# Norm factors of a retention and HGRN2 layer: spread by transposes of a step-zero column in place of products of ones with diagonals

## The chip, the cores and the metric

The kernel runs on one core of one Trainium2 chip. The metric is the device time of one execution in microseconds; the median of several runs counts.

## The reference

One decoder layer for a prompt of 2048 tokens and for 8 decode rows, model width 1024, all in f32. Cut to what matters:

```python
def rmsnorm(x, g):
    y = x * lax.rsqrt(jnp.mean(x * x, axis=-1, keepdims=True) + NORM_EPS)
    return y * g

h = rmsnorm(x, norm_g)                       # one factor per token, one gain per column
p = h @ w_in                                 # 1024 x 4096
rq, rk, rv, rg, hq, hf, hi, hgate = jnp.split(p, 8, axis=-1)
# retention: rotary on rq and rk, fixed decay per head, 4 heads of 128
# HGRN2: forget gate from hf and hg_lb, 4 heads of 128
# both: chunkwise recurrence, norm per head, times silu of the gate
y = x + concat([o_ret, o_hg]) @ w_out
y_prompt, y_sample = rmsnorm(y, final_norm_g)      # and the new states
```

The edited code deals with the factor `rsqrt(mean(x*x) + eps)` of the first norm.

## The kernel before, in words

**Blocks.** The prompt is cut into 8 blocks of 256 tokens, in the order `V_ORDER = [4, 5, 6, 7, 2, 3, 0, 1]`. A first phase runs over `TOK`: the 8 blocks three times, for three sets of weight columns. Its step `i` works on block `TOK[i]`. Steps 0 and 1 are plain products, whose outputs are scaled with the factors; from step 2 on `v_pair(i, after)` computes seven products of a Strassen-like scheme (`PRODUCTS`, `CHAIN`) on sums of input and weight quarters. Every f32 product is made of three on a high and a low part (`three`), and `hi_lo` makes these parts: ScalarE copies the high part (L115), VectorE subtracts it (L116). Later phases (the projections `pj`, the scan and the output projection) are not edited.

**The factors.** The tokens' squares are summed by ScalarE (`stats_sum`, tiles `xn`), and GpSimd makes the factors out of them (`stats_end`, `rsqrt_mean`, L111 and L112): `rs_all` holds them with the 128 tokens of a half block on the partitions, one column for each half block. The input `x_t`, however, lies with the model width on the partitions and the tokens along the row. To scale it, each factor must stand on all 128 partitions, along the row. This is the spread:

- `spread_dg(i)`: VectorE scales the identity with each of the block's two factor columns (L288), into two diagonals `dg` in a buffer `rk`.
- `spread(i)`: TensorE multiplies a matrix of ones with each diagonal (L293), into a PSUM tile `prs`; VectorE copies that to `rb` (L295).
- `tok_ops(i)`: VectorE multiplies the raw input with the gain and with `rb` (L313), `hi_lo` splits it into the operands `ab_h` and `ab_l`, the sums `S` for the scheme are made, and the scaled input and sums are stored (`a_dram`, `s_dram`) for the later steps.

Blocks that a step finds stored (`spooled`) need no spread: eight steps have one, i = 2 to 7, 10 and 11. The spread of step `i + 1` runs while step `i` computes: the diagonals after its first product, the products with ones after its second.

The 8 decode rows have the same in small: `decode_dg` makes an 8x8 diagonal `dgd` (L621), `decode_spread` multiplies ones with it (L625, tile `prsd`). The decode gates' products (`wg_decode`, tiles `pgd`, L600) stand in steps 2 to 5 and use raw weights `wgr` that SyncE's queue loads (L527).

**Order.** Only TensorE runs in the order in which the program writes its instructions:

```python
with tile.TileContext(nc) as tc, tc.manual_schedule(engines={mybir.EngineType.PE}):
```

The order on the other engines and on the DMA queues is planned when the program is built. `behind(f)` and `tc.issue_after` tie some pieces to what stands before them: `past(i, f)` issues the diagonals behind the last VectorE instruction of the block's split (`lows[i]`). Most loads and stores go through SyncE's one queue. The lists `after[n]` say after which product of a step a piece of side work is written.

The query transposes `q_flip` (L470, tile `pqt`) are ordinary transposes on TensorE, four for each half block, and are left as they are.

Of the kernel before, what the change touches and what calls it, by code (L numbers as in the profile page):

```python
# [10 lines left out]
F32 = mybir.dt.float32  # L11
# [3 lines left out]
ALU = mybir.AluOpType  # L15
# [3 lines left out]
P = 128  # L19
# [4 lines left out]
NB = 8  # L24
NH = 4
CH = HALF // P
GW = 512
# [14 lines left out]
def step_kernel(ctx, tc, a, out):  # L42
    nc = tc.nc
    pe, act, dve, pool, sp = nc.tensor, nc.scalar, nc.vector, nc.gpsimd, nc.sync

    const = ctx.enter_context(tc.tile_pool(name="const", bufs=1))
    sm = ctx.enter_context(tc.tile_pool(name="sm", bufs=2))
# [27 lines left out]
    ident = const.tile([P, P], F32, name="ident")  # L75
    make_identity(nc, ident)
    ones = const.tile([P, P], F32, name="ones")
# [27 lines left out]
    rs_all = const.tile([P, T // P], F32, name="rs_all")  # L105
    rsd = const.tile([NB, 2], F32, name="rsd")
# [7 lines left out]
    def hi_lo(h, l, src):  # L114
        act.activation(h, src, AF.Copy)  # L115
        dve.tensor_tensor(l, src, h.bitcast(F32), op=ALU.subtract)  # L116
# [7 lines left out]
    def behind(f):  # L124

        last = {}
        for i in reversed(nc.cur_bb.bb.instructions):
            if i.engine in (dve.engine, act.engine, sp.engine) and i.engine not in last:
                last[i.engine] = i
                if len(last) == 3:  # L130
                    break
        with ExitStack() as es:
            for i in last.values():
                es.enter_context(tc.issue_after(i))
            f()
# [63 lines left out]
    TOK = V_ORDER + [1, 2, 4, 5, 3, 6, 7, 0] + list(range(8))  # L199
    N_V = len(V_ORDER)  # L200
    vctx = ExitStack()
    vq = vctx.enter_context(tc.tile_pool(name="vq", bufs=1))
# [43 lines left out]
    def spooled(i):  # L246
        return i >= 2 * N_V or (i >= N_V and TOK[i] not in TOK[:2])

    def same(i):
        return 0 < i < len(TOK) and TOK[i] == TOK[i - 1]  # L250

    def slot(i):
        return (i - sum(same(n) for n in range(i + 1))) % 2
# [25 lines left out]

    spread_to = {}  # L280

    dgs = {}

    def spread_dg(i):
        t = vq.tile([P, GW], F32, tag="rk", name=f"dg{i}")
        dgs[i] = [t[:, :P], t[:, P : 2 * P]]
        for dg, c in zip(dgs[i], (2 * TOK[i], 2 * TOK[i] + 1)):
            dve.tensor_scalar(dg, ident, rs_all[:, c : c + 1], None, op0=ALU.mult)  # L288

    def spread(i):  # L290
        pt = ps_tr.tile([P, 2, P], F32, tag="tr", name=f"prs{i}")
        for j, dg in enumerate(dgs[i]):
            pe.matmul(pt[:, j], ones, dg, start=True, stop=True)  # L293
        dst = vq.tile([P, GW], F32, tag="rq", name=f"rb{i}")[:, :256]
        dve.tensor_copy(dst, pt.rearrange("p a b -> p (a b)"))  # L295
        spread_to[i] = dst

    sop, lows = {}, {}

    def past(i, f):  # L300
        if i not in lows:
            return f()
        with tc.issue_after(lows[i]):
            f()

    def tok_ops(i, held=None):
        store = held.append if held is not None else lambda f: f()
        r0, r1 = xr[i]
        for j, r in enumerate((r0, r1)):
            if not spooled(i):  # L310
                for k in range(4):
                    kk = 4 * j + k
                    dve.scalar_tensor_tensor(  # L313
                        r[:, k], r[:, k], g_in[:, kk : kk + 1], spread_to[i], op0=ALU.mult, op1=ALU.mult
                    )
            kk = slice(4 * j, 4 * j + 4)
            bb = (slice(3 * slot(i), 3 * slot(i) + 1), slice(3 * slot(i) + 1, 3 * slot(i) + 3))[j]
            ra = r.rearrange("p k (o t) -> p o k t", t=P)[:, : 1 + j]
            hi_lo(ablk[0][:, bb], ablk[1][:, bb], ra)
            if not spooled(i):  # L320
                store(lambda kk=kk, r=r: sp.dma_start(a_dram[TOK[i]][:, kk], r))
        if spooled(i):
            return
        lows[i] = next(x for x in reversed(nc.cur_bb.bb.instructions) if x.engine == dve.engine)
        a11, a21, a12, a22 = r0[:, :, :P], r0[:, :, P:], r1[:, :, :P], r1[:, :, P:]
        ta, tb = (rawp.tile([P, 2, 4, P], F32, tag="raw", name=f"S{n}_{i}") for n in range(2))
        s2, s3, s1, s4 = ta[:, 0], ta[:, 1], tb[:, 0], tb[:, 1]
        dve.tensor_tensor(s1, a21, a22, op=ALU.add)
        dve.tensor_tensor(s2, s1, a11, op=ALU.subtract)
        dve.tensor_tensor(s3, a11, a21, op=ALU.subtract)  # L330
        dve.tensor_tensor(s4, a12, s2, op=ALU.subtract)
        sraw[i] = (ta, tb)
        for n, t in enumerate(sraw[i]):
            store(lambda n=n, t=t: sp.dma_start(s_dram[TOK[i]][n], t))
# [3 lines left out]
    def s_split(i, m):  # L338
        hl = split(sraw[i][m].rearrange("p s k t -> p (s k t)"), f"s{i}{m}")
        for n, op in enumerate((("S2", "S3"), ("S1", "S4"))[m]):  # L340
            sop[i, op] = [
                x[:, n * 512 : n * 512 + 512].rearrange("p (k t) -> p k t", k=4) for x in hl
            ]
# [175 lines left out]
    def wv_comb(k):  # L519
        for op, r in w_sums(wr[k], wr[k + 4]):  # L520
            h, l = wv(op, k)
            hi_lo(h, l, r)
# [92 lines left out]
            dve.tensor_scalar(t, t, rsd[:, ty : ty + 1], None, op0=ALU.mult)  # L615
            sp.dma_start(vd_dram[ty], t)

    dgd = sm.tile([NB, NB], F32, tag="dgd", name="dgd", bufs=1)

    def decode_dg():  # L620
        dve.tensor_scalar(dgd, ident[:NB, :NB], rsd[:, 1:2], None, op0=ALU.mult)  # L621

    def decode_spread():
        pt = ps_tr.tile([P, NB], F32, tag="tr", name="prsd")
        pe.matmul(pt, ones[:NB, :], dgd, start=True, stop=True)  # L625
        rb = sm.tile([P, NB], F32, tag="rbd", name="rbd", bufs=1)
        act.activation(rb, pt, AF.Copy)
        dve.tensor_tensor(xs, xs, rb.unsqueeze(1).to_broadcast([P, KT, NB]), op=ALU.mult)
# [61 lines left out]
    tok_load(2)  # L690
    wv_comb(2)
    wv_comb(3)
    spread_dg(2)
    for ty in (1, 0):
        for c in range(2):
            ps = bank([P, GW], f"pv1{c}{ty}")
# [21 lines left out]
    rk, rb_of = {}, {}  # L718
# [199 lines left out]
    for i in range(2, n_tok):  # L918
        after = {n: [] for n in range(7)}
        m, j = i // N_V + 1, i % N_V  # L920
# [11 lines left out]
        if same(i + 1):  # L932
            for op in ("S1", "S2", "S3", "S4"):
                sop[i + 1, op] = sop[i, op]
        elif i + 1 < n_tok:
            if not spooled(i + 1):
                after[0] += [lambda i=i: past(i, lambda: spread_dg(i + 1))]
                after[1] += [lambda i=i: spread(i + 1)]
            tied = behind if i >= N_V - 1 else lambda f: f()
            late = 2 if same(i) else 0  # L940
            after[2 + late] += [
                lambda i=i, t=tied: t(lambda: tok_ops(i + 1)), lambda i=i, t=tied: t(lambda: s_split(i + 1, 0))
            ]
            after[4 + late // 2] += [lambda i=i, t=tied: t(lambda: s_split(i + 1, 1))]
# [11 lines left out]
            after[4] += [lambda i=i: rot_load(i + 1)]  # L956
        if i == 2:
            after[3] += [lambda: behind(decode_values_out)]
            after[0] += [decode_dg]
            after[2] += [decode_spread]  # L960
        if m < 3:
            if 2 <= j < 6:
# [727 lines left out]
    def op_load(i):  # L1690
        oraw[i] = [rawp.tile([P, 8, P], F32, tag="raw", name=f"or{c}") for c in (2 * i, 2 * i + 1)]
        for c, r in zip((2 * i, 2 * i + 1), oraw[i]):
            sp.dma_start(r, o_dram[:, :, c * P : (c + 1) * P].rearrange("h p t -> p h t"))
# [12 lines left out]
    def op_s12(i):  # L1706
        a11, a12, a21, a22 = op_views(i)
        ta, tb = (rawp.tile([P, 2, 4, P], F32, tag="raw", name=f"oS{n}_{i}") for n in range(2))
        osum[i] = (ta, tb)
        dve.tensor_tensor(tb[:, 0], a21, a22, op=ALU.add)  # L1710
        dve.tensor_tensor(ta[:, 0], tb[:, 0], a11, op=ALU.subtract)

    def op_s34(i):
        a11, a12, a21, a22 = op_views(i)
        ta, tb = osum[i]
        dve.tensor_tensor(ta[:, 1], a11, a21, op=ALU.subtract)  # L1716
        dve.tensor_tensor(tb[:, 1], a12, ta[:, 0], op=ALU.subtract)
# [11 lines left out]
    def op_a(i):  # L1729
        op_pair(i, oraw[i][0], "A11", "A12")  # L1730
# [148 lines left out]
    for n in range(4):  # L1879
        i, st_ = ((4, 0), (4, 4), (5, 0), (5, 4))[n]  # L1880
        wd_at[i] += [(st_, lambda n=n: wd_load(2 * n)), (st_, lambda n=n: wd_load(2 * n + 1))]
        i, st_ = ((4, 3), (5, 0), (5, 4), (6, 1))[n]
# [5 lines left out]
    for i in range(p0, n_pairs):  # L1888
        after = {}
        if i + 1 < n_pairs:  # L1890
            after = {
                0: [lambda i=i: op_load(i + 1)],
                1: [lambda i=i: op_a(i + 1)],
                2: [lambda i=i: op_s12(i + 1)],
                3: [lambda i=i: op_s34(i + 1)],
                4: [lambda i=i: op_s23(i + 1)],
                5: [lambda i=i: op_s14(i + 1), lambda i=i: xr_load(i + 1)],
                6: [lambda i=i: op_a22(i + 1)],
            }
# [88 lines left out]
```

## Time and profile before

| | |
|---|---|
| median of 3 runs | 1039.06 us (1038.57 to 1042.16) |
| the profiled execution | 1038.73 us, span 1037.0 us |
| TensorE busy | 1023.4 us (99%), weight loads 849.9 us (82%) |
| VectorE busy | 746.6 us (72%) |
| ScalarE busy | 556.5 us (54%) |
| GpSimd busy | 129.0 us (12%) |
| moved by DMA | 255.61 MB, mean 247 GB/s |
| diagonals on VectorE (L288) | 16, 0.265 to 0.289 us each, at 46.3 to 221.9 us |
| products with ones (L293) | 32 records, 0.272 to 0.275 us each, at 49.7 to 227.8 us |

Rows of the timeline give the start, the duration, the engine, the line, the operation, the output and the inputs, and the number of merged instructions; in brackets stands the engine's idle time before it and what ended that. PE is TensorE, PEld its weight loads, DVE VectorE, ACT ScalarE, POOL GpSimd, SP SyncE; a q behind the name is the engine's queue. The durations on TensorE overlap, since it is pipelined: the time that an instruction takes from the stream is seen in the start times. A row of a group by line or tile gives the least, the median and the largest duration in ns. A row of the list of waits gives who waited for whom, the total in us, how often, and the longest.

### The profile page before, as it was taken

What the parts mean: (1) busy time and instruction counts of PE and PEld (TensorE: products, weight loads), DVE (VectorE), ACT (ScalarE), POOL (GpSimd) and SP (SyncE); (2) the same over time, 40 slices, a digit from 0 to 9 for tenths busy, and PEclk for the clock granted to TensorE, in tenths of its full rate; (3) what the DMA queues carried; (4) which work ended last, traced back from release to release, by engine and by line L of the source; (5) the groups of instructions that cost most, each with busy time, mean ns of one, the idle gap of its engine ahead of it and who ended that gap; (6) DMA issues with size and microseconds to landing.
All of it is one profiled execution on the core that took longest, in us unless ns stands there. A gap on an engine that the chain in (4) does not pass through costs nothing. (4 is left out here: it accounts for less than half of the span.)

```text
span 1037.0 us, 21324 instructions
## 1 busy us (share of the span) xinstructions
PE 1023.4 (99%) x8231; PEld 849.9 (82%) x8231; DVE 746.6 (72%) x1387; ACT 556.5 (54%) x1217; POOL 129.0 (12%) x231
## 2 busy tenths in 40 slices
PE   9999999999999999999999999999999999999997
PEld 7777778887778888888888889898888878888775
DVE  6886676887666876666665767768768577667886
ACT  7863346644445765545554756566656465433232
POOL 0310001000000111111111100111012102311122
PEclk9999999999999999999999999999999999999999
DMA  8699999779998975586885686745783395575652
GB/s 295 217 326 327 341 326 314 272 250 328 316 333 295 374 241 162 161 276 210 238 256 163 244 313 225 257 138 187 230 266 122 118 370 203 178 271 190 238 184 102
DMA packets 151270, 255.61 MB, mean 247 GB/s; under 512 B 11424, under 2 KB 79280, under 8 KB 151040
## 3 DMA queue, kind: packets, MB, share of 16 engines
q1 hardware_dynamic: 143584, 229.22, 65.6%
q0 software_dynamic: 7440, 24.76, 6.2%
q8 instruction: 65, 1.06, 0.4%
q14 instruction: 37, 0.30, 0.1%
q10 hardware_dynamic: 144, 0.26, 0.1%
HBM read 166.51 MB, written 87.69 MB: 245 GB/s over the span
## 5 line engine op out<-in xcount | busy, mean ns | idle before, releaser
L1235 ACT ACTIVATE kepth<-kh 128x1024 f32<-128x1024 f32 x24 | 25.5, 1061 | 70.4 <-DVE kh L1225 70.4
L1039 PE MATMUL pjfh<-xh,w_h 128*128 128x512 f32 (+2 forms) x160 | 59.5, 372 | 0.0
L1039 PE MATMUL pjqh<-xh,w_h 128*128 128x512 f32 (+2 forms) x160 | 59.0, 368 | 0.0
L1039 PE MATMUL pjqh<-xh,w_l 128*128 128x512 f32 (+2 forms) x160 | 55.7, 348 | 0.0
L1039 PE MATMUL pjfh<-xl,w_h 128*128 128x512 f32 (+2 forms) x160 | 55.7, 348 | 0.0
L1039 PE MATMUL pjqh<-xl,w_h 128*128 128x512 f32 (+2 forms) x160 | 55.6, 347 | 0.1
L1039 PE MATMUL pjfh<-xh,w_l 128*128 128x512 f32 (+2 forms) x160 | 55.6, 348 | 0.0
L1225 DVE TENSOR_TENSOR kh<-kh,fph 128x512 f32<-128x512 f32 x48 | 33.3, 695 | 23.0 <-PE plh L1255 13.2
L116 DVE TENSOR_TENSOR ab_l<-xr,ab_h 128x512 fp32r<-128x512 f32 (+1 forms) x40 | 37.5, 954 | 7.1 <-ACT ab_h L115 6.8
L782 DVE SCALAR_TENSOR_TENSOR obr<-por,omr,rg 128x128 f32<-128x128 f32 x64 | 18.0, 344 | 32.4 <-POOL omr L774 32.4
L772 ACT ACTIVATE obr<-por 128x128 f32<-128x128 f32 x64 | 16.9, 278 | 43.2 <-PE por L759 40.9
L115 ACT ACTIVATE ab_h<-xr 128x512 fp32r<-128x512 f32 (+1 forms) x40 | 32.4, 840 | 13.6 <-DVE xr L313 13.6
L419 ACT ACTIVATE vo<-vo 128x512 f32<-128x512 f32 x32 | 20.1, 630 | 27.3 <-DVE vo L413 13.4
L1039 PEld LDWEIGHTS pjqh<-xh,w_h 128*128 128x128 f32 x160 | 30.4, 190 | 4.6 <-issue 1.2
L1039 PEld LDWEIGHTS pjfh<-xh,w_h 128*128 128x128 f32 x160 | 30.2, 189 | 4.1 <-issue 0.4
L1039 PEld LDWEIGHTS pjqh<-xh,w_l 128*128 128x128 f32 x160 | 30.1, 188 | 4.2 <-issue 0.3
L1039 PEld LDWEIGHTS pjfh<-xh,w_l 128*128 128x128 f32 x160 | 30.1, 188 | 4.0
L1228 DVE TENSOR_TENSOR qqh<-qqh,fph 128x512 f32<-128x512 f32 x48 | 32.8, 684 | 0.0
L1039 PEld LDWEIGHTS pjqh<-xl,w_h 128*128 128x128 f32 x160 | 30.2, 189 | 2.9
L1039 PEld LDWEIGHTS pjfh<-xl,w_h 128*128 128x128 f32 x160 | 30.2, 189 | 2.7
L313 DVE SCALAR_TENSOR_TENSOR xr<-xr,g_in,rb 128x256 f32<-128x256 f32 x64 | 27.1, 480 | 7.1 <-issue 4.3
L1666 PE MATMUL py<-woh,oc_h 128*128 128x512 f32 x64 | 26.7, 417 | 0.0
(1840 smaller groups left out, 3383.1 us busy)
## 6 DMA issues: line engine op xcount, KB each, us to landing
xr<-a_dram SPq DMA_DIRECT2D x24, 512.0 KB, 5.2
S<-s_dram SPq DMA_DIRECT2D x24, 512.0 KB, 5.8
xn<-in_x_prompt SPq DMA_DIRECT2D x32, 256.0 KB, 3.5
xr<-in_x_t SPq DMA_DIRECT2D x16, 512.0 KB, 5.7
a_dram<-xr SPq DMA_DIRECT2D x16, 512.0 KB, 4.1
s_dram<-S SPq DMA_DIRECT2D x16, 512.0 KB
wgr<-in_w SPq DMA_DIRECT2D x16, 512.0 KB, 8.3
xr<-a_dram SPq DMA_DIRECT2D x32, 256.0 KB, 4.4
```

What stands on the lines that cost most here:

```text
L115: act.activation(h, src, AF.Copy)
L116: dve.tensor_tensor(l, src, h.bitcast(F32), op=ALU.subtract)
L313: dve.scalar_tensor_tensor(r[:, k], r[:, k], g_in[:, kk : kk + 1], spread_to[i], op0=ALU.mult, op1=ALU.mult)
L419: act.activation(o, src, AF.Silu)
L772: act.activation(o[:, cc], po[:, h], AF.Square, scale=P ** -0.5, accum_out=ms[:, h : h + 1])
L782: dve.scalar_tensor_tensor(o[:, cc], po[:, h], ms[:, h : h + 1], rb_of[c, "g"][:, cc], op0=ALU.mult, op1=ALU.mult)
L1039: pe.matmul(ps, ww[:, kk], x[:, k, b0 : b0 + n], start=(k == 0 and i == 0), stop=(k == KT - 1 and i == 2),)
L1225: dve.tensor_tensor(kv[:, :, 0, :], kv[:, :, 0, :], two[:, :, 1:2].to_broadcast([P, nb, b]), op=ALU.mult)
L1228: dve.tensor_tensor(qv[:, :, 1, :], qv[:, :, 1, :], two[:, :, 0:1].to_broadcast([P, nb, b]), op=ALU.mult)
L1235: act.activation(ss[:, 512:], k[:, :HALF], AF.Copy)
L1666: pe.matmul(ps, o[:, kk], w[:, k % 4, i * 512 : (i + 1) * 512], start=(k == 0 and n == 0), stop=(k == KT - 1 and n == 2),)
```

## The change

The diagonals go, on VectorE and in the buffers, with the helper that ordered them. The spread becomes two transposes on TensorE. Each reads one column of `rs_all` 128 times over, with a step of zero, as a 128x128 operand, and has the identity as the other operand. The transposed matrix holds the 128 factors along the row, on every partition. The decode factors are spread in the same way from a column of 8. The places in TensorE's order stay.

```diff
-    dgs = {}
-
-    def spread_dg(i):
-        t = vq.tile([P, GW], F32, tag="rk", name=f"dg{i}")
-        dgs[i] = [t[:, :P], t[:, P : 2 * P]]
-        for dg, c in zip(dgs[i], (2 * TOK[i], 2 * TOK[i] + 1)):
-            dve.tensor_scalar(dg, ident, rs_all[:, c : c + 1], None, op0=ALU.mult)
-
     def spread(i):
         pt = ps_tr.tile([P, 2, P], F32, tag="tr", name=f"prs{i}")
-        for j, dg in enumerate(dgs[i]):
-            pe.matmul(pt[:, j], ones, dg, start=True, stop=True)
+        for j in range(2):
+            c = 2 * TOK[i] + j
+            pe.transpose(pt[:, j], rs_all[:, c : c + 1].to_broadcast([P, P]), ident)
         dst = vq.tile([P, GW], F32, tag="rq", name=f"rb{i}")[:, :256]
         dve.tensor_copy(dst, pt.rearrange("p a b -> p (a b)"))
         spread_to[i] = dst
 
-    sop, lows = {}, {}
-
-    def past(i, f):
-        if i not in lows:
-            return f()
-        with tc.issue_after(lows[i]):
-            f()
+    sop = {}
...
-        lows[i] = next(x for x in reversed(nc.cur_bb.bb.instructions) if x.engine == dve.engine)
...
-    dgd = sm.tile([NB, NB], F32, tag="dgd", name="dgd", bufs=1)
-
-    def decode_dg():
-        dve.tensor_scalar(dgd, ident[:NB, :NB], rsd[:, 1:2], None, op0=ALU.mult)
-
     def decode_spread():
         pt = ps_tr.tile([P, NB], F32, tag="tr", name="prsd")
-        pe.matmul(pt, ones[:NB, :], dgd, start=True, stop=True)
+        pe.transpose(pt, rsd[:, 1:2].to_broadcast([NB, P]), ident[:NB, :NB])
...
-    spread_dg(2)
...
-                after[0] += [lambda i=i: past(i, lambda: spread_dg(i + 1))]
                 after[1] += [lambda i=i: spread(i + 1)]
...
-            after[0] += [decode_dg]
```

## The prediction

> **What bounds the kernel now.** I read the page first, then the table by stages, then TensorE's list of waits, and last the timeline around the edited places.
>
> ```profile
> span 1037.0 us, 21324 instructions
> PE 1023.4 (99%) x8231; PEld 849.9 (82%) x8231; DVE 746.6 (72%) x1387; ACT 556.5 (54%) x1217; POOL 129.0 (12%) x231
> ...
> 50.00:100.00 50.00, 48.83 (x238) 37.46 (x237) 40.30 (x71) 24.26 (x46) 3.41 (x6) 1.00 0.92 318
> 100.00:150.00 50.00, 49.51 (x246) 39.29 (x245) 32.51 (x58) 21.10 (x40) 3.25 (x9) 1.00 0.97 344
> 150.00:230.00 80.00, 80.00 (x364) 65.71 (x363) 61.15 (x94) 43.33 (x60) 4.58 (x8) 1.00 0.79 284
> 230.00:500.00 270.00, 269.61 (x1456) 223.81 (x1456) 186.33 (x340) 142.98 (x314) 22.58 (x35) 1.00 0.79 267
> ...
> 800.00:1037.00 237.00, 228.48 (x1871) 185.98 (x1869) 170.09 (x278) 103.66 (x228) 46.72 (x97) 0.99 0.59 204
> ```
>
> The stage rows give start and end, length, busy time of TensorE, its weight loads, VectorE, ScalarE and GpSimd, then granted clock, DMA share and GB/s. TensorE is busy in 1023.4 of 1037.0 us at full clock and has the largest busy time in each stage shown: the kernel is bound by TensorE's instruction stream. So an instruction taken from TensorE counts in full unless TensorE then waits; one taken from VectorE (72%) counts only where TensorE waits for VectorE. All edited code runs between 46 and 229 us. In its first two thirds the DMA engines are 92 and 97% busy, which matters below.
>
> **The products.** Eight spreads run, for token blocks 2 to 7, 10 and 11, and one small one for the decode rows. The view by tile shows the spread's factors, and beside them the query transposes as a price for the new operation:
>
> ```profile
> L293 PEld LDWEIGHTS prs<-dg,ones x32: 187/191/192, 49.7 to 227.8; 128*128 128x128 f32 x32
> L293 PE MATMUL prs<-dg,ones x32: 272/274/275, 49.9 to 227.9; 128*128 128x128 f32 x32
> L470 PEld LDWEIGHTS pqt<-ident,vo x64: 138/139/143, 199.5 to 356.5; 128*128 128x128 f32 x64
> L470 PE MATMUL pqt<-ident,vo x64: 270/272/273, 199.7 to 356.6; 128*128 128x128 f32 x64
> ```
>
> Eight spreads hold 16 products and leave 32 records: two for each f32 product. The 16 groups of query transposes hold 64 transposes and leave 64 records: one each. So a spread goes from four records to two. The durations overlap, so the price is read from start times in the stream:
>
> ```profile
> 83.91 0.39 PE L360 MATMUL pv3b<-wv_l,ab_h 128*128 128x512 f32 x1
> 84.14 0.40 PE L360 MATMUL pv3b<-wv_h,ab_l 128*128 128x512 f32 x1
> 84.37 0.61 PE L293 MATMUL prs<-dg,ones 128*128 128x128 f32 x4
> ...
> 85.05 0.39 PE L360 MATMUL pv3a<-T2l,s30h 128*128 128x512 f32 x1
> ...
> 199.48 0.39 PE L360 MATMUL pv8a<-T4h,ab_l 128*128 128x512 f32 x1
> 199.71 0.60 PE L470 MATMUL pqt<-ident,vo 128*128 128x128 f32 x4
> ...
> 200.38 0.40 PE L360 MATMUL pv8a<-T4l,ab_h 128*128 128x512 f32 x1
> ```
>
> A 512-column product starts 0.23 us after the one before (83.91 to 84.14). From 84.14 to 85.05 lie two such steps and four records: 0.91 - 0.46 = 0.45 us, 0.113 a record. Four transposes cost 0.90 - 0.46 = 0.44 us (199.48 to 200.38), 0.110 each. A spread with two transposes costs 0.22: a saving of 0.23 us, eight times 1.84 us.
>
> The decode factors have the same form with 8 rows:
>
> ```profile
> 66.03 0.39 PE L360 MATMUL pv2a<-T2h,s20l 128*128 128x512 f32 x1
> 66.35 0.38 PE L625 MATMUL prsd<-dgd,ones 8*128 8x8 f32 x2
> ```
>
> Two records become one. I price the one that goes like the others, 0.11 us; the late start (66.35 and not 66.26) stays, since the shape stays. Sum on TensorE: 1.84 + 0.11 = 1.95 us.
>
> The new operand has a step of zero: one column is read 128 times as the stationary operand. No row shows TensorE doing that. The nearest is VectorE, where a multiplication by a column with step zero in its last dimension and an addition of two full tiles take the same time:
>
> ```profile
> L855 DVE TENSOR_TENSOR dv<-dv,dk 128x1024 f32<-128x1024 f32 x8 | 9.7, 1216 | 0.0
> L866 DVE TENSOR_TENSOR dS<-dS,dv 128x1024 f32<-128x1024 f32 x4 | 4.9, 1217 | 0.0
> ```
>
> So I take the ordinary transpose's 0.11 us. The lower bound of a transpose is nothing (saving 0.45 a spread, 3.6 in all); the upper is a load that nothing hides and that takes four of the 0.139 us loads, 0.56 us, kept for the rivals.
>
> One rule of the skill goes further. The Trainium skill, "TensorE: Matmul & The Clock Gate", Terms, calls the transpose mode four times faster for FP32; by it a spread would fall from 0.45 to 0.11 us and the sum would be about 2.8 us instead of 1.95. The records above show a factor of two, 0.22 against 0.45, and the sum goes by them.
>
> **VectorE.** Sixteen scalings of the identity and one of the 8x8 corner go:
>
> ```profile
> L288 DVE TENSOR_SCALAR dg<-ident,rs_all x16: 265/282/289, 46.3 to 221.9; 128x128 f32<-128x128 f32 x16
> L621 DVE TENSOR_SCALAR dgd<-ident,rsd x1: 249/249/249, 48.5 to 48.5; 8x8 f32<-8x8 f32 x1
> ...
> DVE dg L288 <- POOL rs_all L112: 9.9, 4, 3.8
> ...
> DVE dgd L621 <- POOL rsd L112: 1.0, 1, 1.0
> ```
>
> That is 16 x 0.282 + 0.25 = 4.8 us of work, and 9.9 + 1.0 us in which VectorE's queue stood behind a factor that GpSimd had not finished. I cost both at nothing: what follows those waits needs the next product or the spread itself, as at 105 us:
>
> ```profile
> 103.90 0.70 POOL L112 TENSOR_TENSOR rs_all<-rs_all,mhalf 128x2 f32<-128x2 f32 x1
> 104.63 0.48 DVE L288 TENSOR_SCALAR dg<-ident,rs_all 128x128 f32<-128x128 f32 x2 [3.77 <-POOL rs_all L112]
> 105.81 0.61 PE L293 MATMUL prs<-dg,ones 128*128 128x128 f32 x4
> 106.07 0.69 DVE L415 TENSOR_TENSOR vo<-pv4b,s 128x512 f32<-128x512 f32 x1 [0.95 <-issue]
> ```
>
> After the scaling VectorE waits another 0.95 us anyway. TensorE now waits for GpSimd directly. What is queued behind that wait is the entire stream, so a late factor would count in full; but the factor is ready at 104.60 and TensorE comes at 105.81, 1.2 us later, and a dependency through VectorE (to 105.11) goes. The lead that TensorE gains before block 5 is at most 3 x 0.23 + 0.11 = 0.80 us, so there is no wait here. If the squares and loads behind the factor came later than now, the cost would start beyond that 0.4 us margin.
>
> **What is swallowed.** TensorE has short stalls in the same stretch, at work that is not tied to its own pace:
>
> ```profile
> 55.02 0.63 ACT L267 ACTIVATE xn<-xn 128x512 f32<-128x512 f32 x1 [1.36 <-DMA xn<-in_x_prompt]
> 55.65 0.61 ACT L115 ACTIVATE ab_h<-xr 128x512 fp32r<-128x512 f32 x1
> 56.32 0.50 PE L360 MATMUL pv2a<-wv_h,ab_h 128*128 128x512 f32 x1 [0.33 <-ACT ab_h L115]
> 63.42 0.19 PEld L360 LDWEIGHTS pv2a<-T2h,s20h 128*128 128x128 f32 x1 [0.30 <-ACT s L400]
> 78.47 0.28 DVE L288 TENSOR_SCALAR dg<-ident,rs_all 128x128 f32<-128x128 f32 x1 [1.15 <-POOL rs_all L112]
> 86.41 0.97 SPq L527 DMA_DIRECT2D wgr<-in_w  x2
> 94.23 0.62 PE L600 MATMUL pgd<-wgr,pk 128*8 128x256 f32 x8 [0.49 <-DMA wgr<-in_w]
> 136.45 0.62 PE L600 MATMUL pgd<-wgr,pk 128*8 128x256 f32 x8 [0.49 <-DMA wgr<-in_w]
> ```
>
> At 56.32 TensorE waits for the split of block 2 (`ab_h`). ScalarE starts that split late because squares for the statistics stand ahead of it and wait 1.36 us for their load: a DMA sets this time. What block 2's spread saves at 50 us is then waited away here, 0.23 us. At 63.42 the next weight load waits 0.30 us for ScalarE's and VectorE's work on the same block, which follows from 56 us: block 3's saving at 62.7 us goes the same way, 0.23 us.
>
> At 94.23 and 136.45 TensorE waits 0.49 us each for decode gate weights whose load was issued long before (86.41 for the first). In a stretch with 92 and 97% DMA share an earlier TensorE does not bring them sooner. Against that, VectorE stands 1.15 us at 78.47 between the sums that free the weight buffers, and that goes. I let the two cancel: nothing more is swallowed, nothing more won. If the waits take all they can, the savings of block 4, of the decode factors and of block 6 go too, 0.23 + 0.11 + 0.23 = 0.57 us. From 150 us on TensorE is busy in 80.00 of 80.00 us and the last spreads keep theirs.
>
> **Sum.** 1.95 - 0.46 = 1.49 us off. The profiled execution took 1038.73 us (span 1037.0 and 1.73 around it), 0.33 below the median of 1039.06. It goes to 1037.24, the median to **1037.6 us**. The likeliest case's own range: 1.95 - 0.46 - 0.57 = 0.92 to 1.95 + 0.49 = 2.44 us off, 1036.6 to 1038.1. No transfer is added or moved by hand; SP's and GpSimd's queues keep their instructions.
>
> **Rivals.**
>
> 1. *Nothing arrives* (0.16). The stream stays 92 to 97% beside DMA up to 150 us, and every saving up to there is waited away; the three left (blocks 7, 10, 11: 0.69 us) are then lost at a later load or split. Time 1038.4 to 1039.1. For it: the four stalls above. Against it: busy 80.00 of 80.00 and 269.61 of 270.00 afterwards, with nothing to absorb them.
>
> 2. *VectorE's freed waits dissolve the stalls* (0.12). If the 9.9 us make buffers free sooner, so that 0.49 + 0.49 + 0.33 + 0.30 = 1.61 us of stalls vanish and nothing is swallowed, the gain is 1.95 + 1.61 = 3.6 us: 1035.5. For it: the 1.15 us between the sums at 78 us. Against it: VectorE idles behind the scaling anyway (0.95 us at 106.07), and the waits named are for DMAs and ScalarE.
>
> 3. *The step-zero load is slow* (0.07), the case on the other side. Place: the 16 weight loads from the factor columns. Up to 0.226 us a transpose (two records) there is no loss. At the bound of 0.56 us it is 16 x (0.56 - 0.226) = 5.3 us more: 1044.4. For it: no row shows TensorE with such an operand. Against it: the VectorE rows, 1216 and 1217 ns.
>
> 4. *The order on the other engines turns* (0.12). Only TensorE's order is written out; the others' is planned anew once 17 scalings are gone. If on ScalarE one more square with its load comes ahead of `ab_h` at 55.65, that is 1.36 + 0.63 = 2.0 us at a place that TensorE waits for: 1037.6 + 2.0 = 1039.6, and 1041 if nothing is saved either. It decides as soon as that load lands after 55.0 us. Nothing in the trace says that it would.
>
> 5. *The clock* (0.01). TensorE can run slower than in the stream: the warm-up products at the start show it.
>
> ```profile
> 1.13 5.91 PE L84 MATMUL wu<-ones 128*128 128x128 f32 x28 [1.13 <-POOL ones L78]
> ```
>
> That is 0.21 us a record against the 0.113 above, near half speed. If it fell back to that for a stretch after each spread, every 0.23 us step there would take 0.43: 2.0 us more for ten steps, 16 us for eight spreads, and 1053.6. The row for 150 to 230 us, with query transposes at 199.71, says 1.00, and the step behind them is 200.38 - 199.71 = 0.67 for four transposes and one product, with no slowing. The Trainium skill, "TensorE: Matmul & The Clock Gate", Part 4: PE-mode transpose, states that the full clock does not engage for transposes because they do not count as busy. By that rule the time would come out as in this case; the trace disagrees for short groups inside a stream (1.00).
>
> **How the numbers follow.** A change of 0.5%, 5.2 us, is about the least that a measurement of this kernel can tell from none. Forecast 0.52, then 0.16, 0.12, 0.07, 0.12 and 0.01. All but the third and the fifth stay within 0.5%. Slower: 0.07 + 0.01 and a little of the fourth, 0.09. Faster by over 5.2 us takes more than all of case 2 (3.6 us), for instance free transposes besides: 0.05 out of its 0.12. Same: 0.86. The range of 1035.2 to 1041.0 holds the forecast, cases 1 and 2 and case 4 up to its end.
>
> **What the changed profile would show.** Right: 16 records on the line of the new transposes with loads near 0.14 us, blocks of 0.22 us, no scaling on VectorE and no wait there for the factors, and a stall at 56 us longer by about 0.2. The forecast is wrong if the transposes' loads last several tenths of a us, if TensorE waits for the factors at a spread, if ScalarE's order around 55 us differs, or if the two waits for the decode gate weights are gone.

## The result and the profile after

The changed kernel takes 1049.89 us (median of 6 runs, 1047.13 to 1054.14), the kernel before 1039.01 us (6 runs, 1036.93 to 1042.16). The ratio is 1.0103, 95% interval 1.0084 to 1.0123: slower by about 11 us, where 1.5 us less was forecast. The profiled execution took 1050.21 us, 11.48 more than that of before.

The page of the changed kernel, its stages (columns as before) and the rows of the new tiles:

```profile
span 1048.4 us, 21272 instructions
...
PE 1030.4 (98%) x8214; PEld 847.7 (81%) x8214; DVE 743.6 (71%) x1370; ACT 556.8 (53%) x1217; POOL 133.8 (13%) x231
...
q8 instruction: 64, 1.05, 0.4%
```

```profile
50.00:100.00 50.00, 48.29 (x230) 36.14 (x229) 38.79 (x66) 25.00 (x48) 4.67 (x8) 1.00 0.91 318
100.00:150.00 50.00, 50.00 (x242) 38.94 (x241) 31.63 (x53) 20.77 (x40) 3.25 (x9) 1.00 0.97 344
150.00:230.00 80.00, 79.18 (x354) 64.10 (x353) 58.34 (x87) 43.23 (x60) 4.58 (x8) 1.00 0.77 276
230.00:500.00 270.00, 268.77 (x1435) 220.69 (x1434) 185.11 (x338) 140.02 (x309) 22.57 (x35) 1.00 0.79 266
```

```profile
L286 PEld LDWEIGHTS prs<-ident,rs_all x16: 133/134/137, 50.9 to 230.0; 128*128 128x128 f32 x16
L286 PE MATMUL prs<-ident,rs_all x16: 270/272/273, 51.1 to 230.1; 128*128 128x128 f32 x16
```

The edited operations behave as the prediction said: 16 records, loads of 0.134 us with the step of zero, and no wait for a factor. The loss does not sit there. In the stage from 230 to 500 us, which holds no edited operation but the last transpose (230.1 us), TensorE handles 1435 matmuls where it handled 1456, and yet it is busy in 268.77 of 270.00 us: it is busy and slower. The busy share cannot show that; start times can. First the kernel before, then the changed kernel, in the same step of the first phase. The two last rows of the changed kernel belong to products of the sums `T` and `s`:

```profile
162.11 0.39 PE L360 MATMUL pv7a<-wv_h,ab_h 128*128 128x512 f32 x1
...
164.83 0.39 PE L360 MATMUL pv7b<-wv_h,ab_h 128*128 128x512 f32 x1
```

```profile
163.14 0.40 PE L346 MATMUL pv7a<-wv_h,ab_h 128*128 128x512 f32 x1
...
165.94 0.40 PE L346 MATMUL pv7b<-wv_h,ab_h 128*128 128x512 f32 x1
...
210.17 0.39 PE L346 MATMUL pv9a<-T2h,s90l 128*128 128x512 f32 x1
...
212.21 0.39 PE L346 MATMUL pv9a<-T2h,s90l 128*128 128x512 f32 x1
```

Between each pair of `pv7` rows lie 12 steps (a step is the time from the start of one product to the start of the next): 2.72 us before, 2.80 after, or 227 and 233 ns a step. Nine steps of `T` with `s` take 2.04 us, 227 ns as before. Over the whole trace, leaving out steps that hold a pause, 901 steps with `ab_h` or `ab_l` went from 227.4 to 233.1 ns on average (+5.1 us), 493 steps of the output projection (`po`) from 227.2 to 230.2 (+1.5), and those of `pj` and `py` by 1 to 2 ns (+1.0); the 977 steps with `s` stayed at 229.0. Together that is 7.6 of the 11.5 us.

The second part is in TensorE's list of waits:

```profile
PE plh L1233 <- issue: 1.7, 1, 1.7
PE pjfh L1017 <- issue: 1.6, 1, 1.6
```

The list of before has one such row:

```profile
PE plh L1255 <- issue: 1.1, 1, 1.1
```

The timeline of the changed kernel around the later wait:

```profile
865.15 0.69 PE L1233 MATMUL plh<-qqh,kh 128*32 128x16 f32 x61
867.50 0.18 PE L1233 MATMUL plh<-qqh,kh 128*32 128x16 f32 x1 [1.66 <-issue]
...
868.55 0.63 PE L1644 MATMUL py<-woh,oc_h 128*128 128x512 f32 x1
868.98 0.63 PE L1644 MATMUL py<-wol,oc_h 128*128 128x512 f32 x1
```

"Issue" means that nothing which the profile shows held the engine. Both waits stand at the end of a burst of 128 records of 16-column products, and each ends shortly after a packet of the instruction queue (q8) has landed: the packet lands at 616.51 us and TensorE goes on at 617.79, and again at 865.86 and 867.50. This is no chance: the traces of all twelve kernels together hold 20 "issue" waits of TensorE of 0.26 to 3.9 us, and each ends 1.2 to 1.6 us behind the landing of such a packet. There are 64 such packets of 16 KB for 16,428 records of TensorE (matmuls and weight loads), some 256 to a packet, and a burst runs through 256 of them in 1.09 us. Behind the later wait, from 868.55 us on, the steps take 0.43 us: the granted clock is 0.5 for 3.41 us. The kernel before has its one wait at 611 us and no drop. That adds 2.2 us of waiting and 1.7 us of half clock. Pace, these waits and the drop make 11.5 us; by this account the saving of the spreads, 1.95 us, has gone into other waits; experiment 6 shows some of them.

### The profile page after: what moved, and what is told of

Same layout as the page of the kernel before. It is cut to its first block, busy times and chain, and to the rows that moved or that the text cites. A ratio compares the mean times of both kernels' runs of the same rounds, so it can differ in the third digit from the quotient of the medians.

```text
span 1048.4 us, 21272 instructions
## 1 busy us (share of the span) xinstructions
PE 1030.4 (98%) x8214; PEld 847.7 (81%) x8214; DVE 743.6 (71%) x1370; ACT 556.8 (53%) x1217; POOL 133.8 (13%) x231
## 4 chain that ended last, share of the span: by engine, by line
PE 80%; DMA 8%; DVE 4%; ACT 4%; issue 2%; POOL 1%; SPq 1%; POOLq 0%; ACTq 0%
PE po L346 11%; PE pjfh L1017 7%; PE pjqh L1017 7%; PE py L1644 4%; PE plh L1233 1%; PE par L724 1%; PE pur L731 1%; PE por L737 1%; DMA T3l<-ws1T 1%; DMA or<-o_dram 1%; PE por L739 1%; PE puh L1104 1%; PE poh L1120 1%; PE pv21a L346 1%; PE pv22a L346 1%
## 5 line engine op out<-in xcount | busy, mean ns | idle before, releaser
L277 POOL TENSOR_TENSOR ms<-ms 128x2 f32<-128x2 f32 x8 | 13.3, 1657 | 119.2 <-ACT xn L267 119.2
```

## The experiments

Three theories are tried. **A, place of the operands:** the tile `dgd` took 32 bytes of each partition. Without it, everything allocated after it on the left side of SBUF, the on-chip memory that TensorE reads, starts 32 bytes lower in the built program (`wv_h` at 6112 and not 6144), while `ab_h` and `ab_l`, on the right side, stay at 204288 and 216576. Products that read one operand from each side are the ones that slowed. **B, instruction packets:** TensorE's stream lost 17 records, so its 16 KB packets end at other places in the bursts. **C** is the prediction's fourth rival: the planned order on the other engines.

### 1. The 32 bytes put back

```diff
+    sm.tile([NB, NB], F32, tag="dgd", name="dgd", bufs=1)
```

> The changed kernel with an unused 8x8 tile in place of the diagonal that went, so that every tile has the address that it had before the change; all instructions and their order stay as in the changed kernel. Theory A (place of the operands: without the 32 bytes per partition of that tile, all tiles of the left side of SBUF lie 32 bytes lower, while ab_h and ab_l on the right side stay, and products that read one operand from each side start every 232 ns instead of every 227): the steps go back to 227 ns, some 8 us of the 10.9 lost come back, and what is left is the stall at 867 us with its half clock, 3.3 us: 1041 to 1042 us. Theory B (instruction blocks: TensorE's stream has 17 records fewer, so the blocks in which its instructions are fetched end elsewhere) and theory C (the planned order on the other engines): no change, 1049 to 1050 us, steps still at 232 ns.

Measured: 1042.27 us (12 runs, 1038.93 to 1046.1; ratio to before 1.0021, interval 1.0002 to 1.004). The steps with `ab` are back at 227.4 ns, and 7.6 us are back. Every engine has the instructions of the changed kernel in the same order: A holds for the larger part.

### 2. The 32 bytes taken from the kernel before

```diff
-    const.tile([P, 168], F32, name="fill")
+    const.tile([P, 160], F32, name="fill")
```

> The kernel before the change with its unused tile `fill` 32 bytes smaller (160 columns for 168), so that the left side's tiles lie 32 bytes lower, as in the changed kernel; all instructions and their order stay as before. Theory A: products with ab_h or ab_l start every 232 ns, about 8 us slower, 1046 to 1048 us. Theories B and C: 1039 us, steps at 227 ns.

Measured: 1047.17 us (6 runs; before 1038.78, ratio 1.0061, interval 1.004 to 1.0083). An unused tile made 32 bytes smaller slows the kernel by 8.4 us between the medians. The steps, counted as above:

```profile
163.64 0.40 PE L360 MATMUL pv7a<-wv_h,ab_h 128*128 128x512 f32 x1
...
166.44 0.40 PE L360 MATMUL pv7b<-wv_h,ab_h 128*128 128x512 f32 x1
```

12 steps, 2.80 us, 233 ns; over the trace the same classes lose 7.5 us. B and C expected 1039.

### 3. Both sides moved

```diff
-    edge.tile([P, 120], F32, name="edge")
+    edge.tile([P, 128], F32, name="edge")
```

> The changed kernel with the unused tile `edge` on the right side 32 bytes larger (128 columns for 120), so that ab_h and ab_l lie 32 bytes lower too: the distance of the two operands is as before the change, counted in 128 bytes, but both lie 32 bytes below where they lay. Theory A in its relative form (the distance of the two operands counts): steps at 227 ns, 1041 to 1042 us. Theory A in its absolute form (each operand's own place counts): steps at 232 ns or slower, 1049 us or more. Theories B and C: 1049 to 1050 us.

Measured: 1045.33 us (12 runs, 1040.7 to 1048.26; ratio 1.0046, interval 1.0028 to 1.0064).

```profile
163.55 0.39 PE L346 MATMUL pv7a<-wv_h,ab_h 128*128 128x512 f32 x1
...
166.27 0.39 PE L346 MATMUL pv7b<-wv_h,ab_h 128*128 128x512 f32 x1
```

12 steps, 2.72 us: the pace is 227 ns again, though every one of these tiles lies 32 bytes off its old place. What counts is the distance between the two operands. The time is 3 us above the 1041 to 1042 expected, and not by the pace: the profiled run, the slowest of the twelve, waits 2.9 us at the end of the burst that has the later wait above, and the clock drops for longer, 6.8 us:

```profile
862.00:866.00 4.00, 1.06 (x49) 0.82 (x38) 1.13 (x3) 0.00 (x0) 0.54 (x1) 0.80 1.10 356
866.00:869.00 3.00, 3.00 (x8) 2.34 (x7) 2.71 (x6) 2.53 (x3) 0.00 (x0) 0.50 1.07 356
```

The DMA share beside it is 1.10 and 1.07. That does not explain the length of the wait: in 1 the wait at this burst is 1.1 us long, and the share in the 4 us around it is 1.03. Why this kernel is 3 us slower than 1, whose stream of instructions is the same, stays open.

### 4. Distances of 64 and 96 bytes

The same edit as in 2, with `fill` at 152 and at 144 columns, one run each.

> As the kernel before with `fill` smaller, but by 64 bytes. Theory A leaves the form open. If only whole multiples of 128 bytes between the two operands are free: steps of 232 ns or more and 1046 us or more. If 64 bytes are the period: 227 ns and 1039 us. If the cost grows with the distance from a multiple: 237 ns and about 1055 us.

> As the kernel before with `fill` smaller by 96 bytes. If the period is 64 bytes: as with 32 bytes, 232 ns and 1047 us. If it is 128 bytes: 232 ns by a constant price or by the distance from the nearest multiple (32 bytes from the other side), 242 ns and over 1060 us by the distance from below.

Measured: 1047.81 and 1044.23 us. Steps with `ab`: 233.2 and 234.0 ns. So 64 bytes are not the period, and for these products the price does not grow with the distance: 32, 64 and 96 bytes cost 6 to 7 ns a step. Where the steps take 227 ns (before, 1 and 3), the operands lie a whole multiple of 512 bytes apart in the built programs (198144 from `wv_h` to `ab_h`, before and in 3). Distances of 128 and 256 bytes off were not tried, so that whole multiples of 128 are free, as the expectation has it, is not shown. The output projection (`po`) holds the other sign: a third of its steps have operands that lie 32, 64 and 96 bytes short of such a multiple (in 2 and in the two kernels here), and they take 233.4, 230.2 and 233.5 ns. So the price is not the same for every distance. The single times differ by their other waits: the first has one of 2.7 us for a load at 456 us, with a clock drop.

### 5. The packets put back, and moved

With 1 as a base, eight tiny products behind the warm-up bring 16 of the 17 records back. (The edits of the warm-up here also change the planned order in some places, among the first 90 instructions of ScalarE and VectorE and, in the first kernel, of SyncE; later it is the same.)

```diff
+    for n in range(8):
+        pe.matmul(wu[:32, :16], ones[:, :32], ones[:, :16], start=True, stop=True)
```

> The first of these kernels (unused 8x8 tile) with eight more 32x16 products behind the warm-up at the start; they leave 16 records, so that the stream of TensorE's instructions stands nearly where it stood before the change. Theory B: the stall of 1.7 us at 867 us and the half clock behind it are gone, 3 us faster than the first, 1038 to 1039 us. Without B: as the first kernel, 1041 to 1042 us.

Measured: 1039.5 us (12 runs, 1037.0 to 1045.21; ratio 1.0006, interval 0.9986 to 1.0027), 2.8 us less than 1, though the single runs of the two overlap widely. In the trace the wait at that burst is gone. But the profiled run was one of two at 1045 and has another behind the burst at 761 us, 3.9 us long, with a drop of the clock behind it:

```profile
PE pjqh L1021 <- issue: 3.9, 1, 3.9
```

```profile
763.00:767.00 4.00, 0.63 (x3) 0.38 (x2) 3.96 (x10) 1.45 (x3) 1.14 (x2) 0.94 0.91 308
767.00:772.00 5.00, 4.50 (x15) 3.61 (x15) 0.16 (x1) 2.28 (x5) 0.57 (x1) 0.50 0.16 61
```

The packet that ends this wait takes 0.94 us, no more than most (the median of the 65 is 0.96), but it starts only at 765.09, 1.5 us after TensorE has stopped. What makes it start late, no run here shows.

The mirror is the kernel before with 16 records less, in the warm-up:

```diff
-    wu = ps_tr.tile([P, P], F32, tag="tr", name="wu")
-    for n in range(14):
-        pe.matmul(wu, ones, ones, start=True, stop=True)
+    wu = ps_tr.tile([P, 3, P], F32, tag="tr", name="wu")
+    for n in (3, 3, 2, 2, 2, 2):
+        pe.matmul(wu[:, :n], ones, ones.unsqueeze(1).to_broadcast([P, n, P]), start=True, stop=True)
```

> The kernel before the change with its 14 warm-up products written as 6 of the same total width, which leave 12 records in place of 28: TensorE's instruction stream then stands within one record of where it stands in the changed kernel; addresses and nearly the whole order stay as before. Theory B: the stall of 1.3 to 3.1 us among the 16-column products near 859 us, which the kernel before does not have and the changed kernel and the first of these kernels have, comes in, in some runs with a stretch at half clock behind it: 1040.5 to 1042.5 us. Without B: 1038.8 us, and no stall there.

Measured: 1045.11 us (7 runs, 1040.28 to 1047.71; ratio 1.0053, interval 1.0035 to 1.0072), more than expected.

```profile
PE plh L1255 <- issue: 3.5, 2, 2.6
...
PE pv2a L360 <- ACT ab_h L115: 1.6, 1, 1.6
```

The wait has come in at the same burst (2.6 us, half clock behind it). The rest is in the early stage: 1.6 us at 57 us for `ab_h`, also followed by 3.4 us at half clock. Whether the new warm-up causes that one is open: as before, `ab_h` comes after squares that wait for their loads, but on ScalarE two weight copies (`T3h`, `T4h`) have changed their places ahead of them.

In the profiles the wait at this burst stands in all four uncut kernels whose stream is 16 or 17 records short (the changed kernel, 1, 3 and the mirror) and in none of the six others.

### 6. The whole change but the saving

On top of 1:

```diff
-        for j in range(2):
+        for j in (0, 0, 1, 1):
...
-        pe.transpose(pt, rsd[:, 1:2].to_broadcast([NB, P]), ident[:NB, :NB])
+        [pe.transpose(pt, rsd[:, 1:2].to_broadcast([NB, P]), ident[:NB, :NB]) for _ in range(2)]
```

> The changed kernel with the unused 8x8 tile and each transpose of a spread issued twice into the same place: four records a spread as before the change, so that addresses, stream position and TensorE's time are those of before; what stays of the change is that VectorE makes no diagonals. Theory B (position of the stream costs the 3.5 us that the first kernel still lost): 1038.5 to 1039 us. Theory C (the order on the other engines, without the diagonals, costs them): 1041 to 1042 us. Against the kernel with the eight extra products (1039.5 us), which has the cheap spreads: by the prediction's saving this one is 1.5 us slower than that; if the saving is waited away, it is the same or faster.

Measured: 1039.27 us (12 runs, 1037.72 to 1042.76; ratio 1.0002, interval 0.9987 to 1.0018). With addresses and packets as before, neither the transposes with a step of zero nor the missing diagonals cost anything. C is not borne out: without the diagonals VectorE and SyncE have another order than before here, and the time is that of before. The order is not in every place that of the changed kernel, which 1 has. This kernel is 3.0 us below 1, which differs from it in the saved records and in this order, and 0.2 us below the first kernel of 5, which has the saving. So the saving does not show in the times, though an interval of 0.2% could hide it. The profile says where it goes. The kernel before, and 1:

```profile
188.70 1.06 ACT L115 ACTIVATE T3h<-T3l 128x1024 fp32r<-128x1024 f32 x1 [1.08 <-DMA T3l<-ws1T]
189.66 1.99 ACT L115 ACTIVATE B22h<-wg1B 128x1024 fp32r<-128x1024 f32 x2
191.56 0.57 ACT L400 ACTIVATE u<-pv8a 128x512 f32<-128x512 f32 x1
```

```profile
188.72 1.06 ACT L115 ACTIVATE T3h<-T3l 128x1024 fp32r<-128x1024 f32 x1 [1.40 <-DMA T3l<-ws1T]
189.68 1.99 ACT L115 ACTIVATE B22h<-wg1B 128x1024 fp32r<-128x1024 f32 x2
191.58 0.58 ACT L386 ACTIVATE u<-pv8a 128x512 f32<-128x512 f32 x1
...
192.21 0.50 PE L346 MATMUL pv8a<-T3h,s70h 128*128 128x512 f32 x1 [0.69 <-ACT u L386]
```

At 190 us the stream of kernel 1 is 0.68 us ahead of before, net of waits at 73 and 115 us that took the rest. ScalarE waits for a load that comes at the same time in both; `u` is ready at 192.1 in both, and TensorE gives the lead back in one wait of 0.69 us.

### 7. The bursts cut

In kernel 1 and in the kernel before, each burst of 128 records is cut in two, the first half some 3 us earlier:

```diff
+        def levels1(li):
+            box["pl"] = ps_lv.tile([P, 2, CH, 16], F32, tag="lv", name=f"pl{name}{li}")
+            small(box["pl"][:, 0], li, box["kept"])
...
+                  (0.24, lambda: levels1(1)), (0.5, lambda: levels1(3)),
```

> The changed kernel with the unused 8x8 tile, and with each of the 16 bursts of 128 records of 16-column products (256 instructions in 1.09 us, one packet of instructions) cut in two, the first half some 3 us earlier among the 512-column products. Theory B in its full form (a burst outruns the fetch of the next packet): the stalls of 0.7 to 4.3 us behind the bursts and the half clock go, 1035 to 1037 us. Theory B by position alone (cutting moves no packet): about 1041 to 1042 us as the first kernel. If the cut itself costs time at the new places: above 1042 us.

> The kernel before the change with the same cut of the bursts. Theory B in its full form: 1037 to 1038 us, without the slower runs of 1042 to 1044 us that the kernel before has now and then. The difference to the kernel with the cut and the cheap spreads is then what the change itself is worth: 1.5 us by the prediction's sum, 0.0 to 0.7 us if the waits for loads take the savings.

Measured: 1047.79 us (6 runs; ratio 1.0093, interval 1.0063 to 1.0122) and 1045.61 us (6 runs; ratio 1.0064, interval 1.004 to 1.0088). The forecasts of 1035 to 1038 us failed; what the first expectation named last, a price of the cut itself, came in. A pair of 32-column halves takes 0.34 us more than a whole burst, which fits that TensorE changes between its shapes twice more; that is 5 us for 16 bursts. A wait near 882 us grows from 0.2 us before to 1.2 and 1.4 us. The rest of the loss is not explained. As for B, the cut kernel before has no "issue" wait at all in its list, as B in its full form says. The cut kernel 1 still has one, 1.9 us at 612 us, so B in its full form, by which cutting removes these waits, is not borne out. The difference of 2.2 us between the two kernels has the wrong sign for a saving; that wait is one part of it, and the rest stays open.

## Why the prediction was wrong

**The part on TensorE's products was right.** Two records a spread, 0.134 us loads, no slow step-zero load (rival 3), no wait for factors, VectorE's work at nothing. Kernel 1, at block 4 of the prediction's example:

```profile
84.34 0.39 PE L346 MATMUL pv3b<-wv_h,ab_l 128*128 128x512 f32 x1
84.57 0.38 PE L286 MATMUL prs<-ident,rs_all 128*128 128x128 f32 x2
...
85.02 0.40 PE L346 MATMUL pv3a<-T2l,s30h 128*128 128x512 f32 x1
```

That is 0.68 us where it was 0.91: each spread gains 0.23 us. The two waits that were to take the first two savings grew as forecast (TensorE's idle time at 56 us from 0.33 to 0.58 us, at 63 us from 0.11 to 0.31).

**What is swallowed was too small.** This step of the sum let two waits for gate weights cancel against VectorE's freed 1.15 us and allowed 0.46 us. The stage from 50 to 230 us, in kernel 6 (long spreads) and in kernel 1 (short ones):

```profile
50.00:230.00 180.00, 178.02 (x843) 141.83 (x842) 131.43 (x209) 88.47 (x146) 12.23 (x23) 1.00 0.87 311
```

```profile
50.00:230.00 180.00, 177.10 (x830) 140.42 (x828) 131.21 (x209) 88.40 (x146) 12.26 (x23) 1.00 0.87 310
```

TensorE idles 1.98 us in the one and 2.90 in the other; in the kernel before it is 1.66, in the first kernel of 5 3.50. From these pairs, 0.9 to 1.8 of the 1.95 us are waited away. Rival 1, "nothing arrives", given 0.16, described this, with the late place right as well (a load and a split near 190 us). "Busy 80.00 of 80.00" was read as "nothing to absorb them"; a lead of 0.7 us was enough to uncover a wait that the profile before could not show.

**The sum left out a term, and that decides the sign.** The change removes 17 instructions on VectorE, 17 records on TensorE and a tile. The prediction priced the durations of the first two and nothing of the tile: when the diagonals go, the place of `dgd` in memory goes with them, and all that lies behind it moves. 32 bytes a partition cost 7.6 and 8.4 us (experiments 1 and 2). No rival held it: they asked which instruction waits, whether the new load is slow and whether the clock falls, and none whether products far from the edit would keep their pace at the full clock. The bound that was missing goes by the number of products: of the 8214 records, about 2000 belong to the kinds that slowed by 1 to 6 ns on average.

**A record taken away was priced by its duration alone.** The place in the stream of instructions is a second price: 2.8 and 3.0 us here (experiments 5 and 6). The row to see it by was there: the "issue" wait of 1.1 us at the end of a burst, in the list of waits of before. The Trainium skill, "Runtime: NRT & Kernel Launch", Instruction fetch mechanics, states that instructions come in 16 KiB blocks of 256 and that crossing a block is mostly hidden, because dispatch is slower than the filling. The blocks agree with this trace (64 packets of 16 KB). That it is hidden does not hold here behind a burst of 256 records in 1.09 us: TensorE waited up to 3.9 us.

**The clock (rival 5) came in by another door.** No transpose slowed it. Idle time at other places was followed by a slower clock, in some runs: 1.66 us of it by 3.4 us at half clock in the changed kernel, and the 1.6 us in the mirror of experiment 5 by as much, while 2.4 us in kernel 6 were not. The Trainium skill, "TensorE: Matmul & The Clock Gate", Why this matters for your kernels, advises no idle gaps above about 3 us; here half clock came after gaps of 1.6 and 1.66 us already.

**The order on the other engines (rival 4)** changed a little and cost nothing that the runs show: kernel 6 has an order other than before on VectorE and SyncE, ScalarE's as before, and the time of before; the first kernel of 5 has another order on all three and is 0.7 us from it.

No version here beats the kernel before: the best with the change are at 1039.27 and 1039.5 us beside 1038.64 and 1038.78.

## What to carry to other kernels

When a change frees or adds a tile, look where the remaining tiles land before costing anything: compare the start-to-start step of the same product in both traces, and keep the distance of a product's two operands as it was (an unused tile of the old size does it). Look for "issue" waits behind bursts of very short instructions; there, adding or removing a few records anywhere earlier can move a wait of 1 to 4 us in or out, so a difference of some us is not the edit's own until the position is put back. A saving in a stretch that looks fully busy can still be waited away if loads set the pace of another engine beside it.

## What the runs showed of the hardware

- The products of `ab` with both operands a whole multiple of 512 bytes apart (in the place within the partition) start every 227 ns; 32, 64 or 96 bytes off, every 233 to 234 ns. It is the distance that counts, not either place: with both operands moved by 32 bytes they start every 227 ns (experiment 3). Whether 128 or 256 bytes off are free, no run here shows. The Trainium skill, "SBUF — State Buffer", Who interferes with whom, gives TensorE two independent read ports, one for the moving operand and one for the weight loads, and has TensorE wait on nobody; by that the distance would not matter. The runs disagree, with 6 ns a product. Whether the two reads are what collides, no run here shows.
- TensorE waits up to 3.9 us for a packet of instructions and goes on 1.2 to 1.6 us after it has landed (20 waits in twelve traces). The DMA share beside it does not tell the length: it is 0.9 to 1.1 at the waits of 2.9 and 3.9 us, and 1.0 at those of 1.1 us in before and in 1. The single runs of one kernel spread over 7 to 8 us (1038.93 to 1046.1 for experiment 1).
- Switching between the 32-column products and the full ones costs about 0.17 us each time (0.34 us for two more changes, experiment 7).
